# Scan tables of a state-space layer: phases as a sum of two small tables, rounding and decay rows on ScalarE

## The chip, the cores and the metric

The kernel runs on one core of a Trainium2 chip (trn2), once per call. The metric is the device time of one execution in microseconds (us). The engines are named as the profile names them: PE is TensorE's matmuls, PEld its weight loads, DVE is VectorE, ACT is ScalarE, POOL is GpSimd, SP is SyncE, which issues most DMAs. Each engine runs its own instructions strictly in the order in which they stand in its queue.

## The reference, cut to what matters

Two layers are applied to 512 latent and 128 context tokens. Each layer has three mixers. The one that matters here is a bidirectional diagonal state-space scan ("S5"), 32 groups of 16 channels, 64 complex states for each group and direction:

```python
mag = exp(lam_re * dt); ang = lam_im * dt
a_re, a_im = mag * cos(ang), mag * sin(ang)
bu = einsum('blgh,gph->blgp', u, bb)
x_t = a * x_{t-1} + bu_t
y = Re(einsum('blgp,ghp->blgh', x, c)) + u * d_skip
y = jax.nn.gelu(y)
y = y * sigmoid(y @ w_glu + b_glu)
```

The long-convolution mixer, the pooling mixer, the gates and the projections are large matmuls that the change does not touch.

## The kernel before, in words

**Tiling of the scan.** Tokens are taken in chunks of 8, so that a scan has 64 latent steps, a boundary column and 16 context steps: 82 columns (`CZ`). The 128 partitions are 64 states times two directions. The 32 groups are worked in 8 blocks of 4 (`GB`). For a block, `s5_gen` (L843) builds what depends on parameters alone and `s5_run` (L919) does the data part.

**What a block does.** `s5_gen` builds the input weights `i0`, `i1` (products on DVE, L853 and L854, the sum on POOL, L855), transposes them on PE (L864), builds the output weights `ow` and `o1` on POOL (L853 to L855 again), makes a short kernel with PE (L884), brings it through `kh` (L886 on ACT, L887 on DVE) to DRAM and back as `mt` (SP queue, L894). Then come the tables of L895 to L916: for every group and column the rotation angle is column index times frequency. To scan real numbers alone, the data is rotated by minus that angle, scanned with the real decay `r8`, and rotated back. L902 (POOL) multiplies the column numbers by the low frequency part, L904 (POOL) makes the decay rows `d0`; on DVE L906 and L908 multiply by the other two frequency parts, L907 rounds to the nearest whole turn, L909 and L910 combine, L911 clips. ACT takes sine and cosine (L913 to L916) into `tt`. The frequency comes in three parts so that 63 times it keeps its low bits.

`s5_run` has PE compute `pz` (L929, L931); DVE rotates it (L938 to L940); POOL writes the initial state into two column sets of `z` (L941, L942); DVE scans (L946, L947) and rotates back (L951 to L953); POOL copies the last state out (L954, L955); PE computes `yp` (L959, L961); then gelu by tanh: square on ACT (L965), two DVE operations (L966, L967), tanh on ACT (L968), a last DVE operation (L969).

**The stage.** The 8 blocks of a layer run together with the projection of the convolution mixer (`conv_u`, L971), whose matmuls (L257 to L259, 48 to a tile of outputs) fill PE. Every weight tile of those is split into a high and a low part: a CAST on ACT (L234), then a subtraction on DVE (L235); results are copied by ACT (L982) and filtered by DVE (L989, L991).

**What sets the order.** The program is written block by block, but the framework schedules it: it plays all instructions through a cost model and writes each engine's queue in the order that comes out, so parts of blocks b, b+1 and b+2 and of the projection stand interleaved. The queues are fixed then; at run time an engine waits at the head of its queue. Tiles come from pools with a fixed number of buffers (`i0`, `i1`, `o1` one each, `mt`, `tt`, `d0` two, `wh`, `wl` three), and a writer waits until the last reader of its buffer is done.

Of the kernel before, what the change touches and what calls it, by code (L numbers as in the profile page):

```python
# [218 lines left out]
class Body:  # L219
# [623 lines left out]
    def s5_gen(self, l, b, S):  # L843
# [51 lines left out]
        tsh = [P, GB, CZ]  # L895
        tt = S.tile([P, 3] + tsh[1:], F32, tag="tt", name="tt", bufs=2)
        w = S.tile(tsh, F32, tag="tw", name="tw", bufs=1)
        w2 = S.tile(tsh, F32, tag="tw2", name="tw2", bufs=1)
        w3 = S.tile(tsh, F32, tag="tw3", name="tw3", bufs=1)
        mb = self.k(C_MT).unsqueeze(1).to_broadcast(tsh)  # L900
        fb = lambda i: self.f8[:, i, gs].unsqueeze(2).to_broadcast(tsh)
# [11 lines left out]
        nc.scalar.activation(tt[:, 1], w2, AF.Sin, scale=s2)  # L913
        nc.scalar.activation(tt[:, 2], w2, AF.Sin, scale=-s2)
        nc.scalar.activation(w, w2, AF.Abs)
        nc.scalar.activation(tt[:, 0], w, AF.Sin, scale=-s2, bias=self.k(C_PI2))  # L916
# [556 lines left out]
```

## Time and profile before

| | |
|---|---|
| runs shown | 1589.46, 1589.26, 1584.7 us; median 1589.26 |
| profiled execution | span 1583.7 us from first to last instruction; no time beside the span is given for it |
| instructions | 28484 |
| PE busy | 1460.2 us, 92% |
| DVE busy | 1179.0 us, 74% |
| ACT busy | 645.1 us, 41% |
| POOL busy | 690.9 us, 44% |
| chain that ended last | PE 64%, DVE 19%, issue 5%, POOL 4%, DMA 3%, SP queue 2%, ACT 2% |

How to read it: "busy" counts an instruction from its start to its end, whether it streams data or is held up inside; PE's ends are modelled. The chain is followed back from the last instruction, at each step to whatever released it. The table is over the whole span; the two layers' scan stages lie at about 120 to 345 us and 875 to 1120 us.

### The profile page before, as it was taken

How to read it: one execution, taken by the hardware profiler on the slowest of the kernel's cores; microseconds unless marked ns; L12 is line 12 of the kernel's file. 1: busy time of each engine (PE TensorE's matmuls, PEld its weight loads, DVE VectorE, ACT ScalarE, POOL GpSimd, SP SyncE). 2: the span in 40 equal slices, each digit the busy share in tenths (PEclk: the TensorE clock that was granted, in tenths of full speed). 3: DMA queues.
4: the chain of work that ended last, by engine and by line, in shares of the span. 5: the costliest groups of instructions: out<-in, count | busy, mean ns of one | idle time of the engine just before them, and what ended most of it. 6: DMA issues, size and time to landing. Idle time of an engine off the chain costs nothing.

```text
span 1583.7 us, 28484 instructions
## 1 busy us (share of the span) xinstructions
PE 1460.2 (92%) x10764; PEld 1390.7 (88%) x10764; DVE 1179.0 (74%) x1964; ACT 645.1 (41%) x1330; POOL 690.9 (44%) x704
## 2 busy tenths in 40 slices
PE   4888887899999999999998878889999999999997
PEld 2568887799999998999997878889999999999996
DVE  6689999965777795555677799998377769766565
ACT  3274333324333443444335543333443334444443
POOL 5926465630344325454322646654115243566411
PEclk8689888999999999999999998889999999999999
DMA  9425212234222334553552431222532213222154
GB/s 319 164 81 124 68 53 61 61 89 142 91 80 79 102 104 150 180 170 139 190 180 89 123 100 53 64 61 70 152 96 75 81 61 120 81 81 83 41 169 154
DMA packets 114945, 173.53 MB, mean 110 GB/s; under 512 B 30360, under 2 KB 54568, under 8 KB 114297
## 3 DMA queue, kind: packets, MB, share of 16 engines
q1 hardware_dynamic: 113433, 165.37, 33.4%
q0 software_dynamic: 1296, 6.19, 1.1%
q8 instruction: 85, 1.39, 0.3%
q14 instruction: 51, 0.42, 0.1%
q10 hardware_dynamic: 80, 0.16, 0.0%
HBM read 150.12 MB, written 21.56 MB: 108 GB/s over the span
## 4 chain that ended last, share of the span: by engine, by line
PE 64%; DVE 19%; issue 5%; POOL 4%; DMA 3%; SPq 2%; ACT 2%; POOLq 0%; DVEq 0%; ACTq 0%
PE mm L259 13%; PE mm L258 13%; PE mm L257 13%; PE mm L329 4%; PE mm L331 4%; PE mm L330 4%; DVE wl L235 2%; PE modp L400 2%; DVE i L854 1%; PE inva L1117 1%; PE invb L1117 1%; DVE i L853 1%; DVE vx L989 1%; DVE kk L947 1%; DVE kk L946 1%
## 5 line engine op out<-in xcount | busy, mean ns | idle before, releaser
L257 PE MATMUL mm<-hhi,wh 128*128 128x320 f32 x1280 | 405.1, 318 | 10.8 <-ACT raw L982 6.9
L259 PE MATMUL mm<-hhi,wl 128*128 128x320 f32 x1280 | 404.9, 319 | 9.5 <-DVE wl L235 9.4
L258 PE MATMUL mm<-hlo,wh 128*128 128x320 f32 x1280 | 404.7, 317 | 4.4 <-DVE hlo L661 3.6
L235 DVE TENSOR_TENSOR wl<-wr,wh 128x512 fp32r<-128x512 f32 x312 | 256.2, 823 | 90.1 <-ACT wh L234 86.7
L234 ACT CAST wh<-wr 128x512 fp32r<-128x512 f32 x312 | 192.6, 618 | 250.6 <-PE mm L258 181.2
L257 PEld LDWEIGHTS mm<-hhi,wh 128*128 128x128 f32 x1280 | 247.2, 193 | 14.4 <-ACT raw L982 7.9
L259 PEld LDWEIGHTS mm<-hhi,wl 128*128 128x128 f32 x1280 | 246.8, 193 | 12.9 <-DVE wl L235 11.9
L258 PEld LDWEIGHTS mm<-hlo,wh 128*128 128x128 f32 x1280 | 247.5, 193 | 6.5 <-DVE hlo L661 4.5
L258 PE MATMUL mm<-mlo,wh 128*128 128x320 f32 x256 | 79.7, 312 | 0.5 <-DVE mlo L238 0.4
L329 PE MATMUL mm<-hhi,wh 128*128 128x320 f32 x256 | 79.9, 312 | 0.0
L331 PE MATMUL mm<-hhi,wl 128*128 128x320 f32 x256 | 79.5, 311 | 0.0
L257 PE MATMUL mm<-mhi,wh 128*128 128x320 f32 x256 | 79.0, 312 | 0.5 <-ACT wh L234 0.5
L259 PE MATMUL mm<-mhi,wl 128*128 128x320 f32 x256 | 78.9, 310 | 0.4 <-DVE wl L235 0.4
L330 PE MATMUL mm<-hlo,wh 128*128 128x320 f32 x256 | 79.2, 309 | 0.0
L235 DVE TENSOR_TENSOR wl<-ws,wh 128x512 fp32r<-128x512 f32 x64 | 54.4, 849 | 32.1 <-ACT wh L234 30.8
L1211 DVE SCALAR_TENSOR_TENSOR mth<-mth,mm 128x320 f32<-128x320 f32 x64 | 31.2, 488 | 54.8 <-PE mm L259 54.8
L234 ACT CAST wh<-ws 128x512 fp32r<-128x512 f32 x64 | 39.7, 620 | 72.8 <-PE mm L330 36.9
L335 DVE TENSOR_TENSOR mth<-mm,mth 128x320 f32<-128x320 f32 x80 | 39.2, 491 | 33.8 <-PE mm L331 17.2
L961 PE MATMUL yp<-w,ow 128*128 128x81 f32 x256 | 45.5, 307 | 17.5 <-DVE w L953 17.4
L331 PE MATMUL mm<-thi,wl 128*128 128x320 f32 x192 | 60.7, 316 | 0.0
L329 PE MATMUL mm<-thi,wh 128*128 128x320 f32 x192 | 60.6, 316 | 0.0
L330 PE MATMUL mm<-tlo,wh 128*128 128x320 f32 x192 | 59.4, 309 | 0.0
(420 smaller groups left out, 4069.0 us busy)
## 6 DMA issues: line engine op xcount, KB each, us to landing
wr<-w_in SPq DMA_DIRECT2D x224, 256.0 KB
wm<-w_mod SPq DMA_DIRECT2D x48, 512.0 KB
wr<-w_out SPq DMA_DIRECT2D x48, 256.0 KB
hd<-hs SPq DMA_DIRECT2D x32, 256.0 KB
hsr<-hd SPq DMA_DIRECT2D x32, 256.0 KB
mt<-kd SPq DMA_DIRECT2D x128, 32.0 KB
wr<-w_br_a SPq DMA_DIRECT2D x16, 256.0 KB
wr<-w_br_b SPq DMA_DIRECT2D x16, 256.0 KB
```

The source lines that it names most:

```text
L234: nc.scalar.copy(hi, src)
L235: nc.vector.tensor_tensor(out=lo, in0=src, in1=hi.bitcast(F32), op=ALU.subtract)
L257: nc.tensor.matmul(ps[i], wh[:, ks], at(hi, k, sl), start=(k == 0), stop=False)
L258: nc.tensor.matmul(ps[i], wh[:, ks], at(lo, k, sl), start=False, stop=False)
L259: nc.tensor.matmul(ps[i], wl[:, ks], at(hi, k, sl), start=False, stop=(k == kt - 1))
L329: nc.tensor.matmul(out, wh[:, ks], xh, start=(k == 0), stop=False)
L330: nc.tensor.matmul(out, wh[:, ks], xl, start=False, stop=False)
L331: nc.tensor.matmul(out, wl[:, ks], xh, start=False, stop=(k == 3))
L335: e.tensor_tensor(out=o, in0=x, in1=y, op=ALU.add)
L400: nc.tensor.matmul(ps[r0:r0 + 32, :], self.cs[:, 2 * hf + q, :], w[:, q, :], start=(hf < 2), stop=(hf >= 2))
L961: nc.tensor.matmul(yp[:, cols], ow[:, r, g].rearrange("p t h -> p (t h)"), w[:, r, g, 0:CW], start=False, stop=(r == 1))
L1117: nc.tensor.matmul(out, yy[:, ri, cs], ww, start=(n == 0), stop=(n == 5))
```

## The change

It rewrites the tables and moves some small work; the results have the same meaning.

- Column m is written as 8a + b. A new function `phases`, called once a layer from `s5_vals`, makes for all 32 groups a table `ph` of 11 + 8 entries, each already reduced by whole turns: four TENSOR_TENSOR, one TENSOR_SCALAR and one more TENSOR_TENSOR on DVE over 32 x 19 = 608 columns. The constant `C_MT` shrinks from 82 to 19 columns.
- In `s5_gen` the angle of a block is then one broadcast sum on DVE (4 x 88 = 352 columns), a rounding on ACT (adding the constant 12582912), and one SCALAR_TENSOR_TENSOR on DVE that leaves the negated remainder. The clip is gone, and so are the two POOL products.
- The decay rows `d0` are four small ACT multiplications, one a group.
- The four state copies of `s5_run` go from POOL to ACT.
- In gelu the constant 0.044715 goes into the scale of the square, and L966 and L967 become one SCALAR_TENSOR_TENSOR.
- `po` shares its buffer with a temporary of `phases`, `zt` of `mlp` one with `q`; tables now have 88 columns, of which the rotations read 82.

```diff
@@ s5_vals
+        self.phases(S, rs[:, 1:4])
...
+    def phases(self, S, f8):
+        v = self.nc.vector
+        sh = [P, G, NA + NBW]
+        mb = self.k(C_MT).unsqueeze(1).to_broadcast(sh)
+        fb = lambda i: f8[:, i].unsqueeze(2).to_broadcast(sh)
...
+        v.tensor_tensor(out=q, in0=mb, in1=fb(0), op=ALU.mult)
+        v.tensor_scalar(q, q, MAGIC, MAGIC, op0=ALU.add, op1=ALU.subtract)
+        v.tensor_tensor(out=self.ph, in0=mb, in1=fb(1), op=ALU.mult)
+        v.tensor_tensor(out=self.ph, in0=self.ph, in1=q, op=ALU.subtract)
+        v.tensor_tensor(out=q, in0=mb, in1=fb(2), op=ALU.mult)
+        v.tensor_tensor(out=self.ph, in0=self.ph, in1=q, op=ALU.add)
@@ s5_gen
-        e.tensor_tensor(out=w3, in0=mb, in1=fb(2), op=ALU.mult)
-        e.tensor_tensor(out=d0, in0=self.k(C_CM).unsqueeze(1).to_broadcast(tsh),
-                        in1=self.r8[:, gs].unsqueeze(2).to_broadcast(tsh), op=ALU.mult)
-        v.tensor_tensor(out=w, in0=mb, in1=fb(0), op=ALU.mult)
-        v.tensor_scalar(w, w, MAGIC, MAGIC, op0=ALU.add, op1=ALU.subtract)
-        v.tensor_tensor(out=w2, in0=mb, in1=fb(1), op=ALU.mult)
-        v.tensor_tensor(out=w2, in0=w2, in1=w, op=ALU.subtract)
-        v.tensor_tensor(out=w2, in0=w2, in1=w3, op=ALU.add)
-        v.tensor_scalar(w2, w2, 0.49999997, -0.49999997, op0=ALU.min, op1=ALU.max)
+        v.tensor_tensor(out=x, in0=self.ph[:, gs, 0:NA].unsqueeze(3).to_broadcast(tsh),
+                        in1=self.ph[:, gs, NA:].unsqueeze(2).to_broadcast(tsh), op=ALU.add)
+        nc.scalar.activation(fl(w), fl(x), AF.Identity, bias=self.k(C_MAG))
+        v.scalar_tensor_tensor(out=fl(w), in0=fl(w), scalar=MAGIC, in1=fl(x), op0=ALU.subtract, op1=ALU.subtract)
+        for g in range(GB):
+            nc.scalar.mul(d0[:, g], self.k(C_CM), self.r8[:, b * GB + g:b * GB + g + 1])
@@ s5_run
-        nc.gpsimd.tensor_copy(z[0:64, :, :, 0], self.st[0:64, :, gs])
-        nc.gpsimd.tensor_copy(z[64:P, :, :, 63], self.st[64:P, :, gs])
+        nc.scalar.copy(z[0:64, :, :, 0], self.st[0:64, :, gs])
+        nc.scalar.copy(z[64:P, :, :, 63], self.st[64:P, :, gs])
...
-        nc.gpsimd.tensor_copy(self.nst[0:64, :, gs], w[0:64, :, :, 81])
-        nc.gpsimd.tensor_copy(self.nst[64:P, :, gs], w[64:P, :, :, 64])
+        nc.scalar.copy(self.nst[0:64, :, gs], w[0:64, :, :, 81])
+        nc.scalar.copy(self.nst[64:P, :, gs], w[64:P, :, :, 64])
...
-        nc.scalar.activation(u, yp, AF.Square)
-        v.tensor_scalar(u, u, 0.044715, 1.0, op0=ALU.mult, op1=ALU.add)
-        v.tensor_tensor(out=u, in0=u, in1=yp, op=ALU.mult)
+        nc.scalar.activation(u, yp, AF.Square, scale=math.sqrt(0.044715))
+        v.scalar_tensor_tensor(out=u, in0=u, scalar=1.0, in1=yp, op0=ALU.add, op1=ALU.mult)
```

Because the order is planned anew, the queues change too. Line numbers of the change are 12 to 20 higher than those of before from `s5_vals` on.

DVE's queue before, in the middle of layer 0's blocks, from the rounding of one block's table to the next block's rotation (`tw` are the table's temporaries, `i` the input weights, `gu` gelu's):

```order
L907 TENSOR_SCALAR tw<-tw 128x328
L909 TENSOR_TENSOR tw_2274<-tw_2274,tw 128x328
L910 TENSOR_TENSOR tw_2274<-tw_2274,tw_2275 128x328
L854 TENSOR_TENSOR i_2204<-bb,pi 128x512 x2
L966 TENSOR_SCALAR gu<-gu 128x324
L911 TENSOR_SCALAR tw_2274<-tw_2274 128x328
L887 SCALAR_TENSOR_TENSOR kh<-cst,par_142,khp 128x16
L967 TENSOR_TENSOR gu<-gu,yp 128x324
```

DVE's queue of the change at the place of a table (L919 is the broadcast sum, L922 the remainder, L873 the input weights, L239 a weight split):

```order
L968 TENSOR_TENSOR w<-w,t_1879 128x656
L919 TENSOR_TENSOR tt<-ph 128x352
L1003 SCALAR_TENSOR_TENSOR vx_1074<-raw,par_142,vx_1074 128x642
L239 TENSOR_TENSOR wl<-wr,wh 128x512
L873 TENSOR_TENSOR i_2043<-bb,pi 128x512 x2
L922 SCALAR_TENSOR_TENSOR tt<-tt 128x352
L1005 SCALAR_TENSOR_TENSOR vx_1074<-raw,par_142,vx_1074 128x642
```

Six table operations and L966 have become two; `kh` (now L907) no longer stands behind a table operation.

POOL's queue before, one block long (`ow` and `o` are output weights, `d` the decay rows):

```order
L941 COPY z<-rsl 64x8
L942 COPY z<-rsl 64x8
L902 TENSOR_TENSOR tw_2275<-cst,rsl 128x328
L854 TENSOR_TENSOR o_2081<-cw,po 128x512 x2
L904 TENSOR_TENSOR d_2134<-cst,rsl 128x328
L954 COPY nst<-w 64x2x4
L955 COPY nst<-w 64x2x4
L855 TENSOR_TENSOR i_2060<-i_2060,i_2061 128x1024
L853 TENSOR_TENSOR ow<-cw,po 128x512 x2
```

and of the change, one block long:

```order
L874 TENSOR_TENSOR o_1788<-cw,po 128x512 x2
L875 TENSOR_TENSOR i_1767<-i_1767,i_1768 128x1024
L873 TENSOR_TENSOR ow<-cw,po 128x512 x2
L875 TENSOR_TENSOR ow<-ow,o_1788 128x1024
L874 TENSOR_TENSOR o_1926<-cw,po 128x512 x2
```

POOL keeps only the weight products and sums.

ACT's queue of the change, where the moved copies stand (`raw` are the projection's results that PE just finished, `wh` the weight CAST, `it` the transposed weights):

```order
L996 COPY raw<-mm 128x320
L238 CAST wh<-wr 128x512
L956 COPY z<-rsl 64x8
L957 COPY z<-rsl 64x8
L996 COPY raw<-mm 128x192
L996 COPY raw<-mm 128x128
L1001 ACTIVATE vx_1074<-raw,par_142 128x642
L925 ACTIVATE d_1978<-cst,rsl 128x82 x4
L238 CAST wh<-wr 128x512
L996 COPY raw<-mm 128x320
L885 COPY it<-trp 128x512 x2
L969 COPY nst<-w 64x2x4
```

The copies into `z` stand behind a copy that waits for PE, and those out of `w` stand ahead of the next weight CAST (behind L970).

## Rows read from the trace of the kernel before

**Rows 1.** Busy time by stretch: us, PE, PEld, DVE, ACT, POOL busy (instructions), PEclk, DMA share, GB/s

```profile
120.00:345.00 225.00, 191.95 (x1738) 182.94 (x1737) 210.10 (x287) 82.57 (x189) 126.37 (x98) 0.91 0.27 75
875.00:1120.00 245.00, 211.19 (x1828) 202.93 (x1829) 218.13 (x315) 98.00 (x226) 141.46 (x114) 0.90 0.28 78
205.00:305.00 100.00, 78.67 (x675) 74.45 (x674) 96.60 (x135) 36.08 (x84) 60.12 (x46) 0.86 0.19 55
308.00:343.00 35.00, 34.66 (x374) 33.58 (x373) 28.77 (x38) 10.96 (x23) 14.67 (x16) 1.00 0.28 81
```

**Rows 2.** Chain of waits in time, layer 0, first pieces of four blocks' `yp`: start, us

```profile
226.91 0.67 PE yp L961 x4
...
306.32 0.60 PE yp L961 x4
...
341.04 0.41 PE yp L961 x4
```

**Rows 3.** Groups by line and shape, DVE, whole span: count | busy us, mean ns | idle

```profile
L909 DVE TENSOR_TENSOR tw<-tw,tw 128x328 f32<-128x328 f32 x16 | 17.0, 1065 | 0.2
L910 DVE TENSOR_TENSOR tw<-tw,tw 128x328 f32<-128x328 f32 x16 | 13.5, 846 | 0.6
L907 DVE TENSOR_SCALAR tw<-tw 128x328 f32<-128x328 f32 x16 | 11.9, 745 | 0.1
L906 DVE TENSOR_TENSOR tw<-cst,rsl 128x328 f32<-128x328 f32 x16 | 11.8, 736 | 0.0
L911 DVE TENSOR_SCALAR tw<-tw 128x328 f32<-128x328 f32 x16 | 10.8, 677 | 0.1
L908 DVE TENSOR_TENSOR tw<-cst,rsl 128x328 f32<-128x328 f32 x16 | 10.8, 674 | 2.5 <-ACT tw L915 2.5
L966 DVE TENSOR_SCALAR gu<-gu 128x324 f32<-128x324 f32 x16 | 9.7, 605 | 13.4 <-ACT gu L965 13.4
```

**Rows 4.** The same view, POOL: the operations that leave it

```profile
L954 POOL COPY nst<-w 64x8 f32<-64x8 f32 x16 | 21.9, 1370 | 49.7 <-DVE w L953 49.7
L902 POOL TENSOR_TENSOR tw<-cst,rsl 128x328 f32<-128x328 f32 x16 | 16.5, 1032 | 25.0 <-DVE tw L910 23.6 <-DVE hlo L655 1.4
L904 POOL TENSOR_TENSOR d<-cst,rsl 128x328 f32<-128x328 f32 x16 | 16.0, 1001 | 35.0 <-DVE kk L947 31.8 <-DVE raw L977 3.2
L942 POOL COPY z<-rsl 64x8 f32<-64x8 f32 x16 | 11.3, 704 | 0.9
L955 POOL COPY nst<-w 64x8 f32<-64x8 f32 x16 | 8.9, 555 | 0.9
L941 POOL COPY z<-rsl 64x8 f32<-64x8 f32 x16 | 8.5, 533 | 45.7 <-DVE z L940 39.5 <-DVE raw L977 6.2
```

**Rows 5.** Instructions in time, DVE, within one block of layer 0: start, us

```profile
252.82 0.49 DVE L908 TENSOR_TENSOR tw<-cst,rsl 128x328 f32<-128x328 f32 x1
...
254.73 2.48 DVE L910 TENSOR_TENSOR tw<-tw,tw 128x328 f32<-128x328 f32 x1
257.13 3.01 DVE L854 TENSOR_TENSOR i<-bb,pi 128x512 f32<-128x512 f32 x2
...
260.84 2.54 DVE L911 TENSOR_SCALAR tw<-tw 128x328 f32<-128x328 f32 x1
```

**Rows 6.** The same stretch, POOL

```profile
250.36 3.41 POOL L954 COPY nst<-w 64x8 f32<-64x8 f32 x1 [3.67 <-DVE w L953]
...
254.22 2.63 POOL L855 TENSOR_TENSOR i<-i,i 128x1024 f32<-128x1024 f32 x1
...
260.69 2.49 POOL L855 TENSOR_TENSOR ow<-ow,o 128x1024 f32<-128x1024 f32 x1
```

**Rows 7.** Longest waits, 175 to 320 us: us in total, times, longest us

```profile
POOL nst L954 <- DVE w L953: 15.5, 5, 3.7
POOL z L941 <- DVE z L940: 13.0, 5, 4.8
```

**Rows 8.** Groups by line and shape, ACT, 120 to 345 us

```profile
L872 ACT COPY bf<-bb 128x128 f32<-128x128 f32 x6 | 1.8, 298 | 0.1
```

More of the change, by code (lines that the diff above doesn't have):

```diff
@@ L35 @@
 CW = 81
+NA = 11
+NBW = 8
+CT = NA * NBW
 EPS = 1e-6
@@ L47 @@
 GELU_C = math.sqrt(2.0 / math.pi)
-C_ID, C_ONE, C_MT, C_CM, C_DM, C_SEL, C_POSR, C_POSC, C_EL, C_ER, C_PI2, C_EPS, C_N = range(13)
+C_ID, C_ONE, C_MT, C_CM, C_DM, C_SEL, C_POSR, C_POSC, C_EL, C_ER, C_PI2, C_EPS, C_MAG, C_N = range(14)
 def _cst_layout():
-    sizes = [P, P, CZ, CZ, H, 2, 4 * 8, 4 * 64, 15, 11, 1, 1]
+    sizes = [P, P, NA + NBW, CZ, H, 2, 4 * 8, 4 * 64, 15, 11, 1, 1, 1]
     offs = np.concatenate([[0], np.cumsum(sizes)])
@@ L78, in constants @@
     cst[:, CO[C_ONE]:CO[C_ONE] + P] = 1.0
-    mt = np.zeros((2, CZ), f32)
+    mt = np.zeros((2, NA + NBW), f32)
     cm = np.zeros((2, CZ), f32)
-    mt[0, 0:64] = np.arange(64)
-    mt[0, 65:82] = np.arange(17)
+    mt[0, 0:NA] = NBW * np.arange(NA)
+    mt[0, NA:] = np.arange(NBW)
     cm[0, 1:64] = 1.0
     cm[0, 66:82] = 1.0
-    mt[1, 0:64] = 63 - np.arange(64)
-    mt[1, 64:81] = 16 - np.arange(17)
+    mt[1, 0:NA] = 63 - (NBW - 1) - NBW * np.arange(NA)
+    mt[1, NA:] = NBW - 1 - np.arange(NBW)
     cm[1, 0:63] = 1.0
     cm[1, 64:80] = 1.0
-    cst[:, CO[C_MT]:CO[C_MT] + CZ] = np.repeat(mt, 64, 0)
+    cst[:, CO[C_MT]:CO[C_MT] + NA + NBW] = np.repeat(mt, 64, 0)
     cst[:, CO[C_CM]:CO[C_CM] + CZ] = np.repeat(cm, 64, 0)
@@ L112, in constants @@
     cst[:, CO[C_EPS]] = EPS
+    cst[:, CO[C_MAG]] = MAGIC
     fmax = 15
@@ L438, in mlp @@
         v = nc.vector
-        zt = F.tile([33, T], F32, name="zt")
+        zt = F.tile([P, T], F32, tag="mlpq", name="zt", bufs=1)[0:33]
         nc.sync.dma_start(zt, I['zT'])
@@ L821, in s5_vals @@
             rs = t
-        self.r8, self.f8, self.st = rs[:, 0], rs[:, 1:4], rs[:, 4:6]
+        self.r8, self.st = rs[:, 0], rs[:, 4:6]
         self.nst = S.tile([P, 2, G], F32, name="nst")
@@ L894, in s5_gen @@
             nc.sync.dma_start(mt[t_ * H:t_ * H + H], kv[0:H, :, (7 - t_) * H:(7 - t_) * H + P])
[L895 to L901, printed above, removed]
@@ L909, in s5_gen @@
-        v.tensor_tensor(out=w2, in0=w2, in1=w, op=ALU.subtract)
-        v.tensor_tensor(out=w2, in0=w2, in1=w3, op=ALU.add)
-        v.tensor_scalar(w2, w2, 0.49999997, -0.49999997, op0=ALU.min, op1=ALU.max)
-        s2 = 6.2831850
[L913 to L916, printed above, removed]
+        tsh = [P, GB, NA, NBW]
@@ new lines, in s5_gen @@
+        fl = lambda a: a.rearrange("p g a b -> p (g a b)")
+        tt = S.tile([P, 3, GB, CT], F32, tag="tt", name="tt", bufs=2)
+        w, x = (tt[:, i].rearrange("p g (a b) -> p g a b", b=NBW) for i in range(2))
+        v.tensor_tensor(out=x, in0=self.ph[:, gs, 0:NA].unsqueeze(3).to_broadcast(tsh),
+                        in1=self.ph[:, gs, NA:].unsqueeze(2).to_broadcast(tsh), op=ALU.add)
+        nc.scalar.activation(fl(w), fl(x), AF.Identity, bias=self.k(C_MAG))
+        v.scalar_tensor_tensor(out=fl(w), in0=fl(w), scalar=MAGIC, in1=fl(x), op0=ALU.subtract, op1=ALU.subtract)
@@ new lines, in s5_gen @@
+        d0 = S.tile([P, GB, CZ], F32, tag="d0", name="d0", bufs=2)
+        for g in range(GB):
+            nc.scalar.mul(d0[:, g], self.k(C_CM), self.r8[:, b * GB + g:b * GB + g + 1])
+        s2 = 6.2831850
+        tf = lambda i: tt[:, i].rearrange("p g c -> p (g c)")
+        nc.scalar.activation(tf(1), fl(w), AF.Sin, scale=-s2)
+        nc.scalar.activation(tf(2), fl(w), AF.Sin, scale=s2)
+        nc.scalar.activation(fl(w), fl(w), AF.Abs)
+        nc.scalar.activation(tf(0), fl(w), AF.Sin, scale=-s2, bias=self.k(C_PI2))
@@ L950, in s5_run @@
         t2 = S.tile(sh, F32, tag="t1", name="t2", bufs=2)
-        v.tensor_tensor(out=f(w), in0=f(kk), in1=tre, op=ALU.mult)
-        v.tensor_tensor(out=f(t2), in0=f(kk)[:, ::-1], in1=f(tt[:, 1:3])[:, ::-1], op=ALU.mult)
+        v.tensor_tensor(out=w, in0=kk, in1=tre, op=ALU.mult)
+        v.tensor_tensor(out=t2, in0=kk[:, ::-1], in1=tim[:, ::-1], op=ALU.mult)
         v.tensor_tensor(out=w, in0=w, in1=t2, op=ALU.add)
-        nc.gpsimd.tensor_copy(self.nst[0:64, :, gs], w[0:64, :, :, 81])
-        nc.gpsimd.tensor_copy(self.nst[64:P, :, gs], w[64:P, :, :, 64])
+        nc.scalar.copy(self.nst[0:64, :, gs], w[0:64, :, :, 81])
+        nc.scalar.copy(self.nst[64:P, :, gs], w[64:P, :, :, 64])
         yp = self.PS.tile([P, 512], F32, tag="b", name="yp", bufs=3)[:, 0:GB * CW]
```

16 lines of the change are left out of this document (9 added, 7 removed).

## The prediction

> **What bounds the kernel now.** Read the busy time by stretch first. Over the whole span PE looks like the bound, but in the two scan stages it is not: of 225 us in layer 0's stage PE is busy for 192 and DVE for 210, of 245 us in layer 1's for 211 and 218 [rows 1]. In the middle of layer 0's blocks, 205 to 305 us, DVE works for 96.6 of 100 us, PE for 78.7, and the granted clock is 0.86 on average, so some of PE's stretches run at 1.2 GHz, after it had stood idle. In the last 35 us of the stage, where no later block's weights and tables are built any more, PE works for 34.7 us at clock 1.00, that is at 2.4 GHz, and DVE for 28.8 [rows 1].
>
> Then read the chain of waits for the pace. From the first `yp` pieces a block takes (306.32 - 226.91) / 3 = 26.5 us while tables are built and (341.04 - 306.32) / 2 = 17.4 us when they no longer are [rows 2]. So with the same projection matmuls in between, PE alone would go at 17.4, and some 9 us a block are DVE's. I count 12 such blocks: six of eight in each layer, since the last two build nothing for later ones.
>
> Last, see in the instructions in time what DVE's time is. A table product of 328 columns takes 0.49 us at 252.82, but from 254.7 on a like sum takes 2.48 us, two products 3.01 us and a clip 2.54 us [rows 5]: in these microseconds POOL runs its large sums, of 2.63 and 2.49 us [rows 6]. It works the other way too: POOL's copy of 64x8 elements lasts 3.41 us while DVE runs a dense row of two-input work [rows 6]. The two engines hold each other up, and the stage is paced by DVE's own work plus that.
>
> **The change, part by part, for one of the 12 blocks.**
>
> *DVE loses seven operations*: the six of the tables and L966. Their means are 1.065 + 0.846 + 0.745 + 0.736 + 0.677 + 0.674 + 0.605 = 5.35 us [rows 3]. All lie on DVE, the engine that sets the pace. **-5.35.** That the fused gelu operation costs what L967 cost needs no term: same operands, same columns.
>
> *DVE gains two*, the broadcast sum and the remainder, 352 columns with two inputs from SBUF. Lower bound 0.49 us each, the undisturbed product [rows 5]; upper bound 1.07, the dearest table operation [rows 3]. I take 0.80, near the mean of the four TENSOR_TENSOR rows (0.83), because POOL's sums stay. **+1.6** (0.98 to 2.14). Rotations that read 82 of 88 columns move as many elements as before; I put this at nothing, DVE being busy by elements.
>
> *POOL loses six operations*: 1.370 + 1.032 + 1.001 + 0.704 + 0.555 + 0.533 = 5.2 us a block [rows 4]. What DVE's other instructions get back of this has no row. It lies between 0 and 5.2. A good part of it is POOL standing still itself (the 3.41 us copy), so I take a quarter, **-1.3**.
>
> *ACT gains* a rounding, four multiplications of 82 columns and four copies, nine instructions. The nearest row is a small copy of 0.298 us [rows 8]: some 2.7 us a block. ACT is busy for 36 of 100 us in the contended stretch [rows 1], so 2.7 in some 22 us are covered as work; if the cover were gone they would cost 2.7. The Trainium skill ("ScalarE: Activation LUTs", Rules for kernel authors) speaks against this part: additions and multiplications belong on VectorE, which is faster per element. By its figures (in "What ACT_TABLE_LOAD costs") the four multiplications with a scale from a column would be an estimated 4 x 0.35 = 1.4 us rather than my 1.2. No run here has shown it; the sum would be the same while ACT has room.
>
> *ACT's order is the dear point.* The scans now wait for ACT to write the state into `z`, and in ACT's queue these copies stand behind a `raw` copy, which waits for PE, and a weight CAST. Lower bound 0, because POOL took time for the copies as well; upper bound 2.6 us, the mean wait of POOL for `z` (13.0 / 5) [rows 7], which ACT could now add as much again. I take **+0.7**, nearer to nothing, because before L941 and L942 took 1.24 us in this place [rows 4]. Behind the copies out of `w` stand weight CASTs and then PE; at first I count that as covered by the three buffers of `wh`.
>
> *SP and the queues.* No DMA is added or taken away. `kh`, which starts the way through DRAM to `mt`, is no longer behind table operations on DVE; this is in the pace already.
>
> Per block -5.35 + 1.6 - 1.3 + 0.7 = -4.35 us: 26.5 goes to 22.2, which is still above PE's 17.4, so DVE remains the bound and the gain counts in full: 12 x 4.35 = 52 us.
>
> *Once a layer.* `phases`: six operations of 608 columns. By 608/328 times 0.49 or 1.07 each is 0.9 to 2.0 us, so 5.4 to 12 us a layer. In layer 0 they are placed among the filter work before the stage; in layer 1 between weight splits at its start, and DVE has 27 us free in that stage [rows 1]. I take **+2** (0 to 12). PE's queue also has 24 projection matmuls fewer inside each stage; they come after it, where PE is full. At 374 PE instructions in 35 us [rows 1] that is 2.2 us a layer; I take **+3** together (0 to 4.5).
>
> Sum: 52 - 2 - 3 = 47 us off the profiled span of 1583.7, so 1536.7. The median of the runs, 1589.26, lies 5.6 us above that span; I carry this over: **1542 us.**
>
> **The rivals.**
>
> *A. DVE and POOL stop meeting, PE becomes the bound.* All bounds on the good side give more than 9 us a block, and PE's 17.4 us caps it: 12 x 9.1 - 5 = 104 us, 1485 us. For it: the last two blocks do run so, with the clock at 1.00. Against it: in those no weights are built at all, while POOL's sums of 2.5 us each stay in the others. Half of the way lies at 1514.
>
> *B. The hold-ups move on.* What a table operation lost inside itself was POOL's time, and the next DVE instruction will lose it instead, since POOL's large products and sums are all still there. Then the seven operations are worth their undisturbed 0.49 us each, 3.4 us, less 1.0 for the two new ones: 2.4 x 12 - 5 = 24 us, 1565 us. With the ACT wait of up to 2.6 us on top the gain would be gone. For B: in [rows 5] DVE's products of weights are hit just like the table work. Against it: POOL has 5.2 us a block less to do. The Trainium skill ("SBUF — State Buffer", SBUF: two separate sides) gives the rule behind B: the port pair that the two engines share is an exclusive lock for a whole instruction, and the loser blocks fully. By that rule the trace agrees where a clip takes 2.54 us.
>
> *C. Slower: ACT becomes the gate.* POOL used to wait for `w` for 15.5 / 5 = 3.1 us and for `z` for 2.6 us at a time [rows 7], and nothing that PE needs stood behind. On ACT, weight CASTs and `raw` copies stand behind. If both waits come onto the path in full, a block gains 4.35 + 0.7 and loses 5.7: 0.65 us more, 12 x 0.65 + 5 = 13 us more, 1602 us. It decides from 12 x (waits) above 57 us, 4.7 us a block. For it: ACT is strictly in order, and PE's clock falls after idle time. Against it: DVE's queue puts `w` long before PE's need, and ACT's present waits of the same kind did not keep DVE from being 96.6% busy.
>
> *D. No change.* The stage is paced by something that the change leaves, the way of `kh` through DRAM: 1589 us. Against it: DVE's 96.6%.
>
> **How the numbers follow.** What a measurement of this kernel can tell from no change is about 0.3%, 4.8 us. Forecast (1525 to 1560) 0.52, A 0.12, B 0.20, C 0.09, D 0.07. Faster by over 0.3% are the forecast, A and B: 0.84. D and a little of C give 0.08 within 0.3%, the rest of C 0.08 slower. The range leaves out C, D and the far part of A (0.04), 0.20 together: from 1510, a little beyond half of the way to A, to 1583, short of no change.
>
> **What would show it.** Right: the stretch in the middle of the blocks has a pace near 22 us a block and DVE still above 90% busy; PE's clock in the two stages rises above 0.91 and 0.90; the stages outside keep their length within 5 us; POOL's busy time falls by about 80 us, ACT's rises by about 40. A shows as a pace near 18 and PE above 95%. B shows as longer means for the weight products L853/L854 and the splits, and a pace near 24. C shows as DVE waiting for ACT's `z` copies and PE for weight CASTs by several us a block. I am wrong if the scans wait for ACT by more than 3 us a block, or if the pace falls by less than 2 us.

## The result: 19 us faster, under half of the forecast

| | median us | runs | span of the profiled run |
|---|---|---|---|
| before | 1589.3 | 1584.7 to 1589.5 | 1583.7 |
| after | 1570.0 | 1568.1 to 1571.3 | 1569.3 |

The ratio is 0.9883, 95% interval 0.9867 to 0.9899: 16 to 21 us. Forecast were 47 us and 1542; the range (1510 to 1583) holds the result, but it lies near rival B (1565). The profiled spans lie 5.6 and 0.7 us below their medians, so the profiles below divide a difference of 14.4 us.

### The profile after

First the page's busy times, then the busy time by stretch, in the windows of [rows 1].

```profile
PE 1447.5 (92%) x10764; PEld 1381.5 (88%) x10764; DVE 1144.9 (73%) x1896; ACT 683.2 (44%) x1474; POOL 624.7 (40%) x608
```

```profile
120.00:345.00 225.00, 201.16 (x1841) 195.44 (x1840) 192.47 (x265) 111.33 (x285) 96.30 (x59) 0.94 0.30 82
205.00:305.00 100.00, 86.64 (x875) 84.11 (x875) 95.83 (x133) 51.68 (x135) 50.56 (x28) 0.93 0.22 62
308.00:343.00 35.00, 35.00 (x314) 34.43 (x313) 20.89 (x29) 11.54 (x28) 5.87 (x6) 1.00 0.29 85
875.00:1120.00 245.00, 215.75 (x1900) 208.51 (x1899) 202.18 (x278) 122.52 (x301) 106.56 (x69) 0.92 0.33 91
```

In the middle of layer 0's blocks DVE is still busy for 95.8 of 100 us, as in [rows 1], PE does 8 us more and its mean clock went from 0.86 to 0.93. Since the blocks finish earlier, fixed windows no longer compare. The next two fences, of before and after, run from the first copy into `ua` to hyena's first `zt` transpose, in both layers.

```profile
110.60:384.00 273.40, 239.31 (x2059) 229.77 (x2058) 232.21 (x323) 107.51 (x242) 136.03 (x114) 0.93 0.31 88
879.40:1150.30 270.90, 237.29 (x2011) 229.48 (x2010) 224.40 (x319) 108.01 (x240) 141.89 (x117) 0.91 0.32 90
```

```profile
120.20:377.20 257.00, 231.69 (x2046) 225.45 (x2045) 203.80 (x280) 124.70 (x309) 98.87 (x65) 0.95 0.33 92
874.80:1135.40 260.60, 231.35 (x2005) 224.11 (x2006) 206.20 (x284) 127.82 (x312) 106.56 (x69) 0.93 0.33 92
```

The stages became 16.4 and 10.3 us shorter. DVE's busy time fell by 28.4 and 18.2: only a part of what DVE saved became time. In the list of waits of layer 0's stage, PE's waits for DVE fell from 21 to 4 us, but those for ACT (`raw`, `it`) and for DMAs rose from 12 to 22. And layer 0's stage starts late: the first `ua` is at 120.2 instead of 110.6. That is the first surprise. The second is what the remaining DVE instructions cost (groups by line and shape, DVE, 120 to 345 us of after):

```profile
L239 DVE TENSOR_TENSOR wl<-wr,wh 128x512 fp32r<-128x512 f32 x40 | 37.7, 946 | 12.5 <-ACT wh L238 12.4
L874 DVE TENSOR_TENSOR i<-bb,pi 128x512 f32<-128x512 f32 x16 | 20.5, 1315 | 2.5 <-POOL i L875 2.4
L1005 DVE SCALAR_TENSOR_TENSOR vx<-raw,par,vx 128x642 f32<-128x642 f32 x12 | 16.9, 1412 | 0.2
...
L922 DVE SCALAR_TENSOR_TENSOR tt<-tt 128x352 f32<-128x352 f32 x8 | 10.4, 1302 | 0.2 <-ACT tt L921 0.2
...
L919 DVE TENSOR_TENSOR tt<-ph 128x352 f32<-128x352 f32 x8 | 4.1, 517 | 0.0
```

The two new operations have the same size and 0.52 us for the sum, but 1.30 us for the remainder. The weight product L874 takes 1.32 us a piece and its twin L873 0.68. Instructions in time show why: DVE and then POOL of after, 249 to 258 us, in layer 0.

```profile
249.60 3.01 DVE L1005 SCALAR_TENSOR_TENSOR vx<-raw,par,vx 128x642 f32<-128x642 f32 x1
253.08 2.47 DVE L874 TENSOR_TENSOR i<-bb,pi 128x512 f32<-128x512 f32 x2
```

```profile
249.40 2.53 POOL L875 TENSOR_TENSOR i<-i,i 128x1024 f32<-128x1024 f32 x1 [12.75 <-DVE i L873]
251.88 3.11 POOL L873 TENSOR_TENSOR ow<-cw,po 128x512 f32<-128x512 f32 x2
255.08 2.74 POOL L875 TENSOR_TENSOR ow<-ow,o 128x1024 f32<-128x1024 f32 x1
```

The sum on POOL began 0.2 us before DVE's `vx` operation, which then takes 3.01 us instead of 0.88. Where table work stood in [rows 5], other DVE work now meets the same sum. Last, the blocks one by one: busy time from one block's first read of `pz` to the next one's, five of the seven such stretches in layer 0 of after (POOL's busy time is the fifth after the length).

```profile
181.70:209.90 28.20, 23.39 (x198) 22.19 (x197) 28.09 (x42) 14.13 (x37) 15.06 (x9) 0.76 0.19 53
209.90:237.10 27.20, 26.11 (x246) 25.27 (x245) 26.72 (x35) 13.48 (x34) 16.50 (x9) 1.00 0.20 60
237.10:256.00 18.90, 15.47 (x166) 15.27 (x167) 18.76 (x28) 11.15 (x32) 6.53 (x4) 0.91 0.26 73
256.00:281.40 25.40, 21.27 (x204) 20.49 (x202) 24.86 (x33) 11.18 (x30) 15.16 (x9) 0.93 0.18 54
281.40:298.80 17.40, 12.70 (x146) 12.26 (x147) 14.46 (x26) 9.66 (x26) 4.66 (x4) 0.90 0.28 79
```

A block does not take 22 us: it takes 25 to 28 where POOL has 15 to 17 us of work, and 17 to 19 where it has 5 to 7. DVE's instructions differ too (42, 35 and 33 against 28 and 26), so these rows alone do not say which of the two sets the length. Layer 0's seven stretches together, before and then after:

```profile
162.80:329.90 167.10, 139.64 (x1327) 132.12 (x1328) 159.44 (x222) 61.57 (x141) 95.78 (x74) 0.89 0.20 59
```

```profile
165.90:317.30 151.40, 131.34 (x1298) 127.03 (x1299) 142.72 (x197) 76.01 (x197) 63.63 (x34) 0.91 0.23 67
```

A block took 167.1 / 7 = 23.9 us on average and now takes 21.6. Here DVE's busy time fell by 16.7 us and the time by 15.7, nearly in full; PE has 29 instructions fewer, because projection matmuls have moved behind the blocks.

### The profile page after: what moved, and what is told of

It is laid out like the page before. It is cut to its first block, busy times and chain, and to the rows that moved or that the text cites. A ratio compares the mean times of both kernels' runs of the same rounds, so it can differ in the third digit from the quotient of the medians.

```text
span 1569.3 us, 28424 instructions
## 1 busy us (share of the span) xinstructions
PE 1447.5 (92%) x10764; PEld 1381.5 (88%) x10764; DVE 1144.9 (73%) x1896; ACT 683.2 (44%) x1474; POOL 624.7 (40%) x608
## 3 DMA queue, kind: packets, MB, share of 16 engines
q8 instruction: 85, 1.39, 0.4%
## 4 chain that ended last, share of the span: by engine, by line
PE 64%; DVE 16%; issue 6%; DMA 5%; POOL 3%; ACT 3%; SPq 2%; POOLq 0%; DVEq 0%; ACTq 0%
PE mm L261 13%; PE mm L262 13%; PE mm L263 13%; PE mm L333 4%; PE mm L335 4%; PE mm L334 4%; DVE wl L239 2%; PE modp L404 2%; PE inva L1131 1%; PE invb L1131 1%; DVE kk L962 1%; DVE kk L961 1%; DVE i L874 1%; DMA wr<-w_in 1%; DMA yr<-yd 1%
## 5 line engine op out<-in xcount | busy, mean ns | idle before, releaser
L263 PE MATMUL mm<-hhi,wl 128*128 128x320 f32 x1280 | 400.1, 315 | 7.4 <-DVE wl L239 7.4
L239 DVE TENSOR_TENSOR wl<-wr,wh 128x512 fp32r<-128x512 f32 x312 | 258.8, 831 | 106.2 <-ACT wh L238 98.6
L875 POOL TENSOR_TENSOR i<-i,i 128x1024 f32<-128x1024 f32 x16 | 45.2, 2822 | 136.7 <-DVE i L873 104.1
L335 PE MATMUL mm<-hhi,wl 128*128 128x320 f32 x256 | 79.4, 310 | 0.0
L239 DVE TENSOR_TENSOR wl<-ws,wh 128x512 fp32r<-128x512 f32 x64 | 54.4, 849 | 31.4 <-ACT wh L238 30.1
L873 POOL TENSOR_TENSOR ow<-cw,po 128x512 f32<-128x512 f32 x32 | 45.9, 1451 | 34.7 <-PE yp L976 34.6
```

The costliest lines, as they stand in the source:

```text
L239: nc.vector.tensor_tensor(out=lo, in0=src, in1=hi.bitcast(F32), op=ALU.subtract)
L263: nc.tensor.matmul(ps[i], wl[:, ks], at(hi, k, sl), start=False, stop=(k == kt - 1))
L335: nc.tensor.matmul(out, wl[:, ks], xh, start=False, stop=(k == 3))
L873: eng.tensor_tensor(out=out[:, r], in0=hb(r), in1=pb(0), op=ALU.mult)
L875: e.tensor_tensor(out=out, in0=out, in1=tmp, op=ALU.add)
```

## The experiments

Theories. **L**: DVE and POOL exclude each other, so a table operation's own price is small, and the stage pays DVE's work plus POOL's (rival B of the prediction). **K**: ACT's strict order took the gain. **S**: DVE's saving counts only in part. **H**: the phases cost the head, the stretch before the first stage. A kernel's change against another is the difference of their ratios to before, times 1588 us. In e5 and in e9 to e11, `O` is the kernel after with one phase product; it leaves out the split of the phases and their first rounding. e6 and e7 leave out work that the results need. The difference of two kernels that are not before carries both intervals, some 4 to 6 us either way. The queues of every run are planned anew, so no run changes an engine or an instruction with the order held fixed.

| run | edit | median us | ratio to before | 95% interval |
|---|---|---|---|---|
| after | | 1570.0 | 0.9883 | 0.9867 to 0.9899 |
| e1 | phases of layer 0 placed later | 1571.2 | 0.9894 | 0.9871 to 0.9917 |
| e2 | before + phases of layer 0 | 1609.1 | 1.0125 | 1.0089 to 1.0161 |
| e3 | after, copies back on POOL | 1568.8 | 0.9878 | 0.9854 to 0.9903 |
| e4 | after, d0 back on POOL | 1578.5 | 0.9944 | 0.9923 to 0.9964 |
| e5 (O) | after, one phase product | 1558.8 | 0.9807 | 0.9779 to 0.9835 |
| e6 | after, `ow` once a layer | 1529.1 | 0.9622 | 0.9590 to 0.9654 |
| e7 | after, tables once a layer | 1557.6 | 0.9798 | 0.9763 to 0.9834 |
| e8 | after, `i` summed by PE | 1587.8 | 1.0002 | 0.9982 to 1.0022 |
| e9 | O, `i` summed on DVE | 1555.0 | 0.9793 | 0.9771 to 0.9815 |
| e10 | O, both sums on DVE | 1526.1 | 0.9611 | 0.9588 to 0.9633 |
| e11 | O, all weight work on DVE | **1498.1** | 0.9436 | 0.9415 to 0.9458 |
| e12 | before + gelu fused | 1593.6 | 1.0032 | 1.0006 to 1.0058 |
| e13 | before + d0, copies on ACT | 1580.8 | 0.9951 | 0.9935 to 0.9967 |
| e14 | before + all weight work on DVE | 1529.5 | 0.9632 | 0.9614 to 0.9650 |
| e15 | after + all weight work on DVE | 1504.6 | 0.9476 | 0.9459 to 0.9494 |

### The phases: e1, e2, e5

```diff
# e1: called in layer() behind load_u for layer 0, reading the copy of rs
-        self.phases(S, rs[:, 1:4])
+        if l:
+            self.phases(S, rs[:, 1:4])
# e2: kernel before; the result is not read
+        self.phases(Q, rs[:, 1:4, 0])
         self.s5_vals(S, 0, pw[:, :, :, 0], rs[:, :, 0])
# e5: in phases(), for its six operations
+        v.tensor_tensor(out=self.ph, in0=mb, in1=fb(0), op=ALU.mult)
```

> The six phase operations of layer 0 read the small copy of rs and are placed behind the h tiles instead of among the filter work. Theory H (these six, run densely beside POOL's chain, cost the head 9 us): the first hhi comes at 92 to 93 us again instead of 100.9, the first ua near 111 instead of 120.2, and about 2 of the 9 us are paid at the stage's start; time 1561 to 1564 us. Rival (the head's 9 us are a reshuffle of the plan, or belong to the order of the rsl copy on ACT): first hhi stays at 99 to 101, 1568 to 1572 us.

> The kernel before with the six phase operations of layer 0 alone added (their result is not read; the small zt tile shares another's place to make room). Theory H: the first hhi moves from 92.1 to about 101 us, the rest stays, 1597 to 1600 us. Rival: they lie beside other work, as forecast, first hhi 92 to 94, 1589 to 1592 us.

> The kernel after with the six phase operations of each layer replaced by one product (the index times the fractional frequency, without the split and without the first rounding). Theory H2 (the six cost the head what the kernel before with them alone showed, and 4.7 us of DVE in layer 1's stage): first hhi 92 to 94 us, first pz 2 to 3 us earlier than after's 164.5, 1560 to 1566 us. Rival (what the head gets back is lost before the first pz, as when they were only moved, and layer 1's lie beside PE's work): 1567 to 1571 us.

Six operations of some 0.8 us cost the kernel before 20 us (1.0125, 14 to 26), far more than theory H gave them. e2 also lets `zt` of `mlp` share another tile's place, as after does, and no run prices that by itself. In after, five of the six in both layers cost 12 us. The trace of after shows how. POOL, then DVE:

```profile
53.52 2.24 POOL L716 TENSOR_TENSOR exo<-exo,ex 128x64 f32<-128x64 f32 x1
...
56.30 1.29 POOL L716 TENSOR_TENSOR exo<-exo,ex 128x64 f32<-128x64 f32 x1
57.68 3.15 POOL L717 TENSOR_SCALAR exo<-exo 128x64 f32<-128x64 f32 x1
...
62.04 0.32 POOL L720 TENSOR_TENSOR exo<-exo,ex 128x64 f32<-128x64 f32 x1
```

```profile
54.80 0.77 DVE L849 TENSOR_TENSOR ph<-ph,phq 128x608 f32<-128x608 f32 x1
...
56.64 0.77 DVE L850 TENSOR_TENSOR phq<-cst,rs 128x608 f32<-128x608 f32 x1
...
68.01 7.45 DVE L239 TENSOR_TENSOR flo<-hc,fhi 128x512 fp32r<-128x512 f32 x1 [6.69 <-ACT fhi L238]
75.39 8.84 DVE L559 SCALAR_TENSOR_TENSOR hc<-hx,hc 128x512 f32<-128x512 f32 x1
```

Beside DVE's row of phases and filter products, POOL's steps of 0.32 and 0.37 us take up to 3.15, so its chain of small steps for the discretisation reaches L720 6 us later (62.04; before, as L716, 56.13). ACT waits 9.06 us for that chain with filter casts queued behind it. Then POOL runs without a gap, and DVE's next two operations, 0.7 us each, last 7.45 and 8.84. Busy times of 62 to 85 us, of before and of after:

```profile
62.00:85.00 23.00, 19.68 (x130) 15.24 (x127) 20.31 (x32) 12.37 (x24) 20.46 (x24) 0.83 0.51 167
```

```profile
62.00:85.00 23.00, 10.68 (x75) 7.99 (x74) 16.99 (x4) 2.85 (x6) 21.52 (x41) 0.67 0.33 97
```

DVE finishes 4 instructions instead of 32, and PE idles for 12 of 23 us. With one product (e5) the first `hhi` comes at 89.0 instead of 100.9 and the first `pz` at 157.1 instead of 164.5. In e1 the first `hhi` came at 93.2, as H expected, but nothing was gained: the last copy into `ua` is at 149.3, as in after (149.0), and in DVE's queue five of the moved operations now stand among the weight splits and tables ahead of it, which is the likely reason, though no run shows it by itself. Moving them gained nothing; making them fewer did.

### ACT and POOL: e3, e4, e13

```diff
# e3: and the same for the two copies out of w
-        nc.scalar.copy(z[0:64, :, :, 0], self.st[0:64, :, gs])
-        nc.scalar.copy(z[64:P, :, :, 63], self.st[64:P, :, gs])
+        nc.gpsimd.tensor_copy(z[0:64, :, :, 0], self.st[0:64, :, gs])
+        nc.gpsimd.tensor_copy(z[64:P, :, :, 63], self.st[64:P, :, gs])
# e4: (e13: the reverse, and e3's reverse, in the kernel before)
-            nc.scalar.mul(d0[:, g], self.k(C_CM), self.r8[:, b * GB + g:b * GB + g + 1])
+        e.tensor_tensor(out=d0, in0=self.k(C_CM).unsqueeze(1).to_broadcast([P, GB, CZ]),
+                        in1=self.r8[:, gs].unsqueeze(2).to_broadcast([P, GB, CZ]), op=ALU.mult)
```

> The kernel after with the copies into z and out of w back on POOL. Theory K (ACT's strict order is what took the gain: PE waits for raw and it copies behind small ACT work): PE's waits for ACT fall from about 11 us a layer to 5, 1562 to 1567 us. Theory L (DVE and POOL hold each other up, each POOL instruction taken away is a gain): four POOL instructions a block come back, copies of 64x8 of up to 3 us, 1572 to 1580 us.

> The kernel after with the decay row d0 as one POOL product of 328 columns again instead of four ACT multiplications of 82 (0.353 us each). Theory K: ACT loses 1.4 us a block ahead of the sines, 1563 to 1567 us. Theory L: POOL gets a product of about 1 us a block back that locks DVE out for its time, 12 times 0.5 to 1 us, 1576 to 1582 us. Neither: 1568 to 1572 us.

> The kernel before with d0 (four multiplications) and the four copies on ACT, tables and gelu as they were: the change's relief of POOL alone. The forecast's terms for it, 12 x (-1.3 + 0.7) = -7: 1580 to 1583 us. Theory L, with what the two single undoings showed in the kernel after (d0 8.5 us, copies nothing): 1577 to 1582 us. If the change's whole gain of 30 us without its phases is POOL's relief: 1558 to 1566 us. If it is all the table work of DVE: 1587 to 1592 us.

The copies are worth the same on either engine (0.9878 against 0.9883): neither K nor L has its price for them. That a small gain on ACT and a small loss on POOL cancel is not excluded. The product d0 costs 10 us on POOL, 0.6 us for each of its 16. The relief by d0 and the copies gives 7.8 us (5.2 to 10.3). The forecast's 7.2 (12 x 0.6) also held a sixth POOL operation, L902, which e13 keeps. It has the size of d0's product (1.03 and 1.00 us in [rows 4]), and no run removes it alone.

### DVE's saving: e7, e12

```diff
# e7: sum, rounding, remainder and sines for b == 0 only; later blocks read its tt
+        if b == 0:
+            tt = self.tt = S.tile([P, 3, GB, CT], F32, tag="tt", name="tt", bufs=1)
...
# e12: kernel before
-        nc.scalar.activation(u, yp, AF.Square)
-        v.tensor_scalar(u, u, 0.044715, 1.0, op0=ALU.mult, op1=ALU.add)
-        v.tensor_tensor(out=u, in0=u, in1=yp, op=ALU.mult)
+        nc.scalar.activation(u, yp, AF.Square, scale=math.sqrt(0.044715))
+        v.scalar_tensor_tensor(out=u, in0=u, scalar=1.0, in1=yp, op0=ALU.add, op1=ALU.mult)
```

> The kernel after with the tables (sum, rounding, remainder, three sines, absolute value) built for the first block of a layer alone: DVE loses 1.8 us and ACT some 2.9 in 14 of 16 blocks, d0 stays. By the forecast's rule that DVE's time counts in full: 14 x 1.8 = 25 us, 1545 us or less. Theory S (only a part of what DVE saves becomes time, 27 of 47 us between the two kernels): 12 to 17 us, 1553 to 1558 us. Theory K: more than DVE's part, since ACT is relieved too, below 1545 us with PE's waits for ACT gone.

> The kernel before with the gelu constant folded into the square alone: DVE loses one operation of 0.605 us a block. The forecast's rule (in full, 12 blocks): 7 us, 1580 to 1583 us. Theory S (about half): 1584 to 1587 us. No effect: 1588 us.

In e7 the 28 operations that fall away had 1.8 us a pair; the time falls by 13 us, half of it, and ACT loses the rounding, the sines and the absolute value as well. In e12 nothing is gained at all; the kernel is 1 to 9 us slower. Busy times of e12, again from first `ua` to first `zt`:

```profile
111.90:386.20 274.30, 238.83 (x2060) 230.74 (x2059) 234.59 (x315) 108.18 (x242) 135.53 (x113) 0.93 0.33 87
881.00:1157.60 276.60, 238.10 (x2016) 231.04 (x2016) 227.65 (x311) 108.72 (x240) 141.48 (x117) 0.91 0.32 88
```

DVE has 8 instructions fewer in each stage and is busy for 2.4 and 3.3 us longer. What one instruction lost to POOL, the others inherited: a table operation, on average 1.07 us in [rows 3], takes 1.58 in e12.

```profile
L909 DVE TENSOR_TENSOR tw<-tw,tw 128x328 f32<-128x328 f32 x16 | 25.3, 1580 | 0.2
```

### POOL's remaining work: e6, e8 to e11, e14, e15

```diff
# e6: kernel after; later blocks read the first block's weights
-        kr(e, ow, o1, self.cw, self.po, 1)
+        if b == 0:
+            kr(e, self.ow, o1, self.cw, self.po, 1)
...
# e8: kernel after; kr leaves out the sum, PE accumulates both halves
-                nc.tensor.transpose(ps[:, g * P:g * P + P], i0[:, r, g].rearrange("p t h -> p (t h)"), self.ident)
+                for q, a in enumerate((i0, i1)):
+                    nc.tensor.matmul(ps[:, g * P:g * P + P], a[:, r, g].rearrange("p t h -> p (t h)"), self.ident,
+                                     start=(q == 0), stop=(q == 1))
# e9 to e11: kernel O; e14: before; e15: after. fin is the engine of the sum
-        def kr(eng, out, tmp, mat, pw, pr):
+        def kr(eng, fin, out, tmp, mat, pw, pr):
...
-            e.tensor_tensor(out=out, in0=out, in1=tmp, op=ALU.add)
+            fin.tensor_tensor(out=out, in0=out, in1=tmp, op=ALU.add)
...
-        kr(v, i0, i1, self.bb, self.pi, 1)
+        kr(v, v, i0, i1, self.bb, self.pi, 1)
...
-        kr(e, ow, o1, self.cw, self.po, 1)
+        kr(v, v, ow, o1, self.cw, self.po, 1)   # e9: (e, e, ...), e10: (e, v, ...)
```

> The kernel after with POOL's output weights ow built for the first block of a layer alone and used for all eight (the other blocks' are left out): POOL loses 8.2 us in 14 of 16 blocks, nothing else changes. Theory L (a block takes DVE's own work plus the time POOL holds it up): the periods of 24 to 28 us between first pz reads go to 16 to 20, PE's 25 to 29 us of idle time a layer nearly vanish, 1520 to 1535 us. Rival K (PE waits for ACT and for mt through DRAM, whatever POOL does): periods stay above 21, 1555 to 1568 us.

> The kernel after with POOL's sum of the two input weight products left out: PE adds them itself, by 16 accumulating matmuls with the identity in place of 8 transposes. POOL loses 2.9 us a block, PE gains 8 matmuls of 128 columns a block, 1 to 2 us. Theory L: DVE is held up less and no longer waits for that sum, 12 x (2 to 3) less PE's share that lies on the path, 1545 to 1560 us. Rival (PE's added work costs what POOL's relief gives): 1565 to 1575 us.

> The kernel with one phase product (1559 us), and the sum of the input weight products on DVE instead of POOL. DVE gains an instruction of 1024 columns, 1.2 us undisturbed, POOL loses one of 2.5 to 2.9. Theory L (the two engines exclude each other, so POOL's undisturbed time adds to DVE's): 12 x (2.5 - 1.2) = 16 us off the loops, about half of it in the end, 1548 to 1554 us; the remainder L922 no longer takes 2.7 us anywhere. The forecast's rule (DVE sets the pace, POOL's relief is worth a quarter of its time): 12 x (1.2 - 0.7), 1561 to 1566 us.

> As the last, with the sum of the output weight products on DVE too: 2.4 us more DVE work a block than in the kernel of 1559 us, 5 us less POOL work. Theory L: half of 12 x 2.6, 1540 to 1550 us. The forecast's rule: 1563 to 1575 us.

> POOL does no weight work in the blocks at all: its four products of 512 columns (1.05 us undisturbed on POOL, 0.65 on DVE) and both sums are DVE's, 5 us more DVE work a block, some 9 us less on POOL. Theory L: 12 x (9.2 - 5.0) = 50 us at most, about half in the end, 1530 to 1545 us, every weight product of DVE at its undisturbed 0.65 to 0.68 us. The forecast's rule: 12 x (5.0 - 2.3) = 32 us more, 1575 to 1592 us.

> The kernel before with all weight products and sums of the blocks on DVE, w3, d0 and copies still on POOL, nothing of the change in it. Theory L (the two engines exclude each other, whatever else is there): the same 61 us as between the kernel with one phase product and its like, 1525 to 1535 us. Rival (only the change's shorter tables made room on DVE; with 7 operations more a block DVE now sets the pace): 1550 to 1590 us.

> The kernel after, with its six phase operations, and all weight products and sums on DVE. Theory H2 (the phases cost the head its 11 us beside POOL's discretisation, which this edit does not touch): 1507 to 1512 us. Rival (they cost it only where DVE is full in the stage): 1497 to 1502 us.

**e6** leaves POOL one operation a block, and 41 us go. What is left shows the exclusion cleanly (POOL, then DVE, same stretch of e6):

```profile
211.52 2.66 POOL L875 TENSOR_TENSOR i<-i,i 128x1024 f32<-128x1024 f32 x1 [15.92 <-DVE i L873]
231.31 2.50 POOL L875 TENSOR_TENSOR i<-i,i 128x1024 f32<-128x1024 f32 x1 [17.14 <-DVE i L873]
```

```profile
211.87 2.69 DVE L924 SCALAR_TENSOR_TENSOR tt<-tt 128x352 f32<-128x352 f32 x1
...
231.06 0.52 DVE L924 SCALAR_TENSOR_TENSOR tt<-tt 128x352 f32<-128x352 f32 x1
```

The same instruction takes 2.69 us if the sum has begun before it, and 0.52 if it begins first. **e8** takes that sum away too, but gives PE 384 instructions more (11148 against 10764) and 31.7 us more busy time: slower by 19 us than after, beyond what either expectation allowed. **e9** gives DVE the sum instead, 1.2 us for 2.5: within the uncertainty of O. **e10** and **e11** go on, and work taken from POOL and given to the engine that looks 95% busy makes the kernel faster: by 31 us against O, and by 28 us more. That is more than L expected (14 and 32 us below its ranges). In e14 the same edit takes 58 us off the kernel before, with nothing of the change in it. First the page of e11, then that of e15, then DVE's groups of e11 over the blocks of both layers:

```profile
PE 1426.2 (95%) x10764; PEld 1358.4 (91%) x10764; DVE 1118.0 (75%) x1982; ACT 683.8 (46%) x1474; POOL 445.9 (30%) x512
```

```profile
PE 1422.8 (95%) x10764; PEld 1358.4 (90%) x10764; DVE 1131.5 (75%) x1992; ACT 681.8 (45%) x1474; POOL 450.0 (30%) x512
```

```profile
L866 DVE TENSOR_TENSOR i<-bb,pi 128x512 f32<-128x512 f32 x32 | 20.7, 682 | 0.0
L866 DVE TENSOR_TENSOR ow<-cw,po 128x512 f32<-128x512 f32 x32 | 20.7, 682 | 0.0
...
L868 DVE TENSOR_TENSOR i<-i,i 128x1024 f32<-128x1024 f32 x16 | 19.4, 1213 | 0.0
```

DVE has 86 instructions more in e11 than in after and is busy for 27 us less; e15, which keeps all six phase operations, has 96 more and is busy for 13 us less. The products take 0.68 us (L874 of after: 1.32), the sums of `i` 1.21 (on POOL 2.82, by the page of after). The phases (e15 against e11) still cost 6 us, within the uncertainty of e5's 12. e11 beats both kernels: 1498.1 us, 5.6% below before; e15, the kernel after in full, is 5.2% below. Where e11's time comes from, in the seven stretches of layer 0:

```profile
159.50:305.10 145.60, 141.77 (x1441) 136.87 (x1439) 142.04 (x235) 80.56 (x208) 9.07 (x8) 1.00 0.28 78
```

The blocks are hardly shorter than after's (20.8 us each), but 143 more PE instructions run in them, at a mean clock of 1.00 instead of 0.91, and both PE and DVE are busy for over 97% of the stretch. So the gain goes with the projection work that the new plan puts beside the blocks, and with the clock. How much a new order alone would give is open.

e14 also gives the table operations' own price. DVE's groups of e14:

```profile
L909 DVE TENSOR_TENSOR tw<-tw,tw 128x328 f32<-128x328 f32 x16 | 8.9, 559 | 0.0
L908 DVE TENSOR_TENSOR tw<-cst,rsl 128x328 f32<-128x328 f32 x16 | 8.3, 517 | 0.8 <-ACT tw L915 0.8
L906 DVE TENSOR_TENSOR tw<-cst,rsl 128x328 f32<-128x328 f32 x16 | 8.0, 502 | 0.0
L910 DVE TENSOR_TENSOR tw<-tw,tw 128x328 f32<-128x328 f32 x16 | 8.0, 501 | 0.2
...
L966 DVE TENSOR_SCALAR gu<-gu 128x324 f32<-128x324 f32 x16 | 5.4, 339 | 20.1 <-ACT gu L965 20.1
L907 DVE TENSOR_SCALAR tw<-tw 128x328 f32<-128x328 f32 x16 | 5.2, 323 | 0.0
L911 DVE TENSOR_SCALAR tw<-tw 128x328 f32<-128x328 f32 x16 | 5.2, 323 | 0.1
```

## Why the prediction was wrong, step by step

- **What bounds the stage** was half right. DVE is busy for 95.8 of 100 us in after too. But its busy time in [rows 1] was not its work: e11 and e15 do POOL's share as well in less. The bound was DVE and POOL together, one at a time where operations like e6's pair meet.
- **"DVE loses seven operations, -5.35"** is the step that failed. The means of [rows 3] were taken as what the stage would get back. In e14 the seven take 0.559 + 0.517 + 0.502 + 0.501 + 0.339 + 0.323 + 0.323 = 3.06 us; the other 2.3 us was time held by POOL. That this part bought nothing is shown by two pairs of runs: the change with one phase product is worth 31 us where the hold-ups are (before to e5) and 31 us where POOL has no weight work (e14 to e11); by the means the first should be some 12 x (5.35 - 1.6 - 2.03) = 21 us the larger (2.03 is the own net price, worked out under the next point). That the next DVE instruction loses the time instead is shown by e12 for one of the seven. In after it does not show as a sum: over the whole span L874 and L1005 take longer than in before (1.39 and 1.23 us; 1.13 and 1.10), L873 and L1003 less by as much (0.74 and 0.98; 0.93 and 1.19). There, of the 28.4 us that DVE saved in layer 0's stage 16.4 became time; the rest became idle time of DVE, nearly all of it outside the seven stretches.
- **"DVE gains two, +1.6"**: 0.52 + 1.30 = 1.82 in layer 0's stage, but in e11, without POOL, 0.516 + 0.514 = 1.03. So the net own price is 2.03 us a block, 12 x 2.03 = 24 us for tables and gelu, where I had 45. Measured, as e5 against e13: 23 us, some 5 either way. That the two agree so well is luck in part, since this difference also holds POOL's L902.
- **POOL's relief, -1.3 + 0.7**: 7 us forecast, 7.8 measured without L902 (e13). That these two terms hold is luck in part: the copies show no price (e3), and d0 alone shows 10 us (e4). POOL's busy time fell by 66 us, not by the 80 that I named as a sign; ACT's rose by 38, as said.
- **"Once a layer, +2 (0 to 12)"**: 12 us for five of six operations in two layers (e5), 20 for one layer in the kernel before (e2). I put them among filter work that would hide them, and costed them at DVE's durations. Their place in layer 0 was beside POOL's chain of small steps, and the price was the head's, not their own 5 us: with one product (e5) the first `pz` comes 7.4 us earlier. An early `hhi` alone does not give it back (e1). The stretch before the stage did not keep its length within 5 us, as I had named: the first `ua` comes 9.6 us later.
- **Displaced projection matmuls, 2.2 us a layer**: from the last `pz` to the first `zt` after takes 60.2 and 58.9 us, before 54.6 and 51.6, so 5.6 and 7.3 us a layer come back there. The direction was right; for both layers I had 3 us, and it is 13.
- The sum by the measured parts: -7.8 - 22.8 + 12.0 = -18.6, which is after's ratio by construction (e13, e5 against e13, after against e5). It is rival B with dearer phases: its 2.4 x 12 = 29 us stand against 7.8 + 22.8 measured, though B had no relief of POOL in it. Its working used the undisturbed 0.49 us, which was in [rows 5]. I gave it 0.20 because POOL would have 5.2 us a block less to do, and put no price on what the 11 us that stay (L873 to L875) do to DVE.
- **Rival C** did not come. DVE's scans wait for ACT's `z` for 0.3 us in layer 0's stage, and e3 shows no gain from taking the copies off ACT. **The clock** rose as said, 0.91 to 0.94 and 0.90 to 0.92. The signs that I named do not decide between the forecast and B. Of the two weight products one became longer and one shorter. The pace fell from 23.9 to 21.6 us, both averages over seven stretches; my 26.5 came from three of the dearer blocks, so neither 22 nor 24 can be held against it. By the same measure the fall is 2.3 us a block, where I had 4.35.

The Trainium skill ("SBUF — State Buffer", SBUF: two separate sides) has the rule by which B would have been the forecast: the port pair is locked for a whole instruction by whichever of the two begins first. e6's pair of 2.69 and 0.52 us agrees. The Trainium skill ("Perfetto Trace Analysis", Optimizing Scalar/DVE Operations) says that moving work between these two might not help; e11 shows the reverse direction paying: here moving it to the engine that looked full gave 59 us (e11 against O).

## What to carry to other kernels

Before an operation is priced by its mean, look at its fastest occurrence and at what the other engine of the pair ran during its slow ones: only the fastest is its own, and here the rest bought nothing when the operation went. If DVE is full and POOL does two-input work beside it, add up both in undisturbed durations; if POOL needs longer for the same tile (here at best 1.05 against 0.68 us for a product, 2.39 against 1.21 for a sum), try the work on DVE, even when DVE seems to have no room. And a small piece of work "hidden" in the head has to be set against the longest chain there, POOL's too.
